# A seven-product GELU matmul kernel: B's operands kept in DRAM, two products of four groups split again, A's rows weighed by ScalarE

**Chip, cores, metric.** One core of a Trainium2 chip. The metric is the device time of one execution in microseconds (us), median of several.

## The reference

```python
def reference(a, b):            # a, b: 4096 x 4096 float32
    x = np.matmul(a, b)
    return 0.5 * x * (1 + np.tanh(np.sqrt(2 / np.pi) * (x + 0.044715 * x**3)))
```

## The kernel before

The kernel forms each 2 x 2 block product with seven products instead of eight (the Winograd form of Strassen's scheme), in f16 with fp32 sums in PSUM. There are 16 groups: four row blocks of A by four column blocks of B. A product is four steps (`q`) of 16 matmuls of 512 columns. Its operands are blocks of A and B, or sums of two, made by DVE two steps ahead.

```python
PRODUCTS = [("M3", "Y", "11", ("12", "22", 1)), ("M5", "X", ("11", "12", -1), "22"), ...]   # 7 of them

def make_sums(gi, s, q):                       # DVE: operand sums, 128 x 2048 f16 each
    ...
    t = pool.tile([P, 4 * NC], F16, name=tag, tag=tag, bufs=AHEAD + 1)      # AHEAD = 2
    nc.vector.tensor_tensor(out=x, in0=y, in1=z, op=...)

def keep(tag, src, bufs):                      # ScalarE copies a finished bank out of PSUM
    t = pool.tile([P, NC], F32, name=tag, tag=tag, bufs=bufs)
    nc.scalar.copy(out=t[:, :], in_=src[:, :])
```

After M5, M7 and M1 the next product goes on adding into the same PSUM banks, so TensorE must wait until ScalarE has copied each bank out (`m`, `x`).

A's rows come through two staging buffers. GpSimd issues the load (fp32 to f16), DVE turns the chunk into `aT`, and the buffer is free.

```python
s = pool.tile([P, NX, RUN], F16, name="stage", tag="stage", bufs=2)          # load_a
nc.vector.transpose(dst[:, :, x, :], src[:, :, x, :])                        # turn_a
```

The scheme is exact enough only for tame inputs, so the kernel also sums the squares of A's rows and B's columns and falls back to plain products if they are out of bounds. Before, ScalarE squared resident tiles and DVE added the squares.

## Time and profile before

| | before |
|---|---|
| time, median of 3 | 1579.29 us |
| span of the profiled run | 1577.1 us |
| TensorE busy, granted clock | 1567.7 us (99%), 0.999 |
| DVE, ScalarE, GpSimd busy | 78%, 33%, 34% |
| TensorE's waits, all added | 4.2 us |

Two more views. First the waits between other engines (columns: engine, tile and line, what it waited for; total us, times, longest).

```profile
POOL stage L186 <- DVE aT L161: 178.0, 16, 56.7
ACT square L207 <- DVE energy L431: 130.7, 96, 4.7
...
DVE aT L161 <- DMA stage<-in_a_dram: 39.9, 14, 10.8
```

A staging buffer is waited for until DVE has turned it, never until ScalarE has done anything. DVE stands 39.9 us in all at turns whose rows are not there, and TensorE does not feel it. Second, the DMA issues (count, size of one, median us from issue to landing).

```profile
bR<-in_b_dram POOLq DMA_DIRECT2D x832, 128.0 KB, 5.2
...
stage<-in_a_dram POOLq DMA_DIRECT2D x112, 256.0 KB, 6.8
```

### The profile page before, as it was taken

The numbers are of one execution on the slowest core, as the hardware profiler recorded it, in microseconds if no ns is written. First come the engines' busy times: TensorE is split into PE (matmuls) and PEld (weight loads), VectorE is DVE, ScalarE is ACT, GpSimd is POOL, SyncE is SP. The second block draws the span as 40 slices with busy tenths as digits, with TensorE's granted clock in tenths as the row PEclk, the third lists the DMA queues.
The fourth block names the chain that finished last, engine by engine and source line by source line (L and its number), as shares of the span: only waits on it lengthen the run. The fifth ranks groups of instructions, "written<-read, shape, count | busy, mean of one in ns | idle before, by whom it ended". The sixth has DMA issues, their size and how long they took to land. (4 is left out here: it accounts for less than half of the span.)

```text
span 1577.1 us, 19678 instructions
## 1 busy us (share of the span) xinstructions
PE 1567.7 (99%) x7246; PEld 709.6 (45%) x7246; DVE 1233.7 (78%) x1381; ACT 518.0 (33%) x710; POOL 537.7 (34%) x980
## 2 busy tenths in 40 slices
PE   9999999999999999999999999999999999999998
PEld 4444444444444444444444444444444444444443
DVE  1698888967787888895778778887687778988775
ACT  1036445311122545531111344542211145364111
POOL 7753442420234144341124413245011443314400
PEclk9999999999999999999999999999999999999999
DMA  9999884882968378686597937679468885747802
GB/s 173 198 215 189 132 162 79 161 162 48 193 106 158 87 131 160 108 179 115 87 161 117 186 72 142 146 113 182 79 121 146 134 160 93 151 105 134 161 28 82
DMA packets 225047, 211.13 MB, mean 134 GB/s; under 512 B 20144, under 2 KB 192176, under 8 KB 224944
## 3 DMA queue, kind: packets, MB, share of 16 engines
q0 software_dynamic: 187648, 142.67, 61.7%
q1 hardware_dynamic: 37296, 67.13, 11.8%
q8 instruction: 59, 0.97, 0.2%
q14 instruction: 44, 0.36, 0.1%
HBM read 285.22 MB, written 67.11 MB: 223 GB/s over the span
## 5 line engine op out<-in xcount | busy, mean ns | idle before, releaser
L331 PEld LDWEIGHTS <-aS 128*128 128x128 f16 x4960 | 485.3, 98 | 587.2 <-issue 2.2
L186 POOL DMA_DIRECT2D bR<-in_b_dram x832 | 447.6, 544 | 700.0 <-DVE bS L302 329.7
L302 DVE TENSOR_TENSOR aS<-aT 128x2048 f16<-128x2048 f16 (+1 forms) x312 | 376.1, 1212 | 151.0 <-PE accX L331 114.5
L331 PE MATMUL accX<-bS,aS 128*128 128x512 f16 x1984 | 431.1, 379 | 0.0
L302 DVE TENSOR_TENSOR bS<-bR 128x2048 f16<-128x2048 f16 x310 | 376.1, 1218 | 69.3 <-PE accX L331 58.5
L331 PEld LDWEIGHTS <-aT 128*128 128x128 f16 x1984 | 194.2, 98 | 234.8 <-issue 0.8
L422 ACT ACTIVATE y<-y 128x512 f32<-128x512 f32 x192 | 118.5, 630 | 351.8 <-DVE y L431 351.4
L331 PE MATMUL accY<-bS,aS 128*128 128x512 f16 x992 | 216.7, 379 | 1.8 <-DVE y L431 1.8
L331 PE MATMUL accY<-bS,aT 128*128 128x512 f16 x992 | 216.9, 379 | 0.5 <-DVE bS L302 0.5
L331 PE MATMUL accX<-bS,aT 128*128 128x512 f16 x992 | 216.7, 379 | 0.0
L331 PE MATMUL accX<-bR,aS 128*128 128x512 f16 x992 | 216.7, 379 | 0.0
L331 PE MATMUL accY<-bR,aS 128*128 128x512 f16 x992 | 216.7, 379 | 0.0
L186 POOL DMA_DIRECT2D stage<-in_a_dram x144 | 89.9, 630 | 249.0 <-DVE aT L161 178.0
L431 DVE TENSOR_TENSOR energy<-energy,square 128x1024 bf16<-128x1024 bf16 x240 | 164.4, 685 | 9.5 <-ACT square L207 5.7
L395 ACT COPY x<-accX 128x512 f32<-128x512 f32 x128 | 74.9, 585 | 224.3 <-PE accX L331 224.3
L207 ACT ACTIVATE square<-aT 128x1024 bf16<-128x1024 f16 x120 | 123.4, 1051 | 70.6 <-DVE energy L431 70.2
L207 ACT ACTIVATE square<-bR 128x1024 bf16<-128x1024 f16 x120 | 123.0, 1050 | 62.5 <-DVE energy L431 60.5
L161 DVE STREAM_TRANSPOSE aT<-stage 128x2048 uint32<-128x2048 uint32 (+1 forms) x37 | 74.6, 2017 | 46.0 <-DMA stage<-in_a_dram 39.9
L395 ACT COPY m<-accX 128x512 f32<-128x512 f32 x60 | 34.7, 579 | 215.7 <-PE accX L331 213.6
L422 ACT ACTIVATE y<-accX 128x512 f32<-128x512 f32 x64 | 38.2, 597 | 100.1 <-PE accX L331 99.9
L431 DVE TENSOR_TENSOR x<-accX,x 128x512 f32<-128x512 f32 x64 | 44.0, 691 | 21.8 <-ACT y L422 19.1
L431 DVE TENSOR_TENSOR y<-accY,m 128x512 f32<-128x512 f32 x60 | 39.9, 687 | 12.5 <-ACT m L395 12.4
(38 smaller groups left out, 344.9 us busy)
## 6 DMA issues: line engine op xcount, KB each, us to landing
bR<-in_b_dram POOLq DMA_DIRECT2D x832, 128.0 KB, 5.2
out_dram<-y SPq DMA_DIRECT2D x256, 256.0 KB, 5.7
stage<-in_a_dram POOLq DMA_DIRECT2D x112, 256.0 KB, 6.8
stage<-in_a_dram POOLq DMA_DIRECT2D x32, 128.0 KB, 5.1
row<-seen_d SPq DMA_DIRECT2D x2, 1.5 KB, 4.2
seen_d<-seen SPq DMA_DIRECT2D x1, 3.0 KB, 7.4
```

What stands on the lines that cost most here:

```text
L161: nc.vector.transpose(dst[:, :, x, :], src[:, :, x, :])
L186: nc.gpsimd.dma_start(out=dst, in_=src)
L207: nc.scalar.activation(t[:, :], src, ACT.Square)
L302: nc.vector.tensor_tensor(out=x, in0=y, in1=z, op=ALU.add if o[2] > 0 else ALU.subtract)
L331: nc.tensor.matmul(acc[:, :], sa[:, j // 2, i * P : (i + 1) * P, j % 2], sb[:, j, :], start=start and j == 0, stop=stop and j == 3, skip_g ...
L395: nc.scalar.copy(out=t[:, :], in_=src[:, :])
L422: nc.scalar.activation(y[:, :], src[:, :], ACT.Gelu_apprx_tanh)
L431: nc.vector.tensor_tensor(out=o[:, :], in0=x[:, :], in1=y[:, :], op=op)
```

## The change

Intent: TensorE is the bound, so take matmuls away. M3 and M5 of groups 11, 13, 14 and 15 become seven products of half size each. That needs DVE time for more sums and joins, so DVE is relieved in two ways: B's operands, once made, are written to DRAM in groups 1 to 5 and fetched from group 6 on; and A's rows are weighed by ScalarE straight from the staging buffer, with no DVE work. The core of the diff:

```diff
+SPLIT_GROUPS = (11, 13, 14, 15)
+CHECK_GROUP = 9
+TURNS = ((2, 2), (3, 1), (5, 2), (6, 1), (7, 0), (7, 3), (8, 2), (9, 1))
...
+    def weigh_rows(mb, quad, c, xs):
+        s = staged[mb, quad, c]
...
+        for x in xs:
+            nc.scalar.activation(
+                weighed[mb, quad, c][:, :RUN], s[:, x, :], ACT.Square, accum_out=weighed[mb, ih][:, k, x : x + 1]
+            )
...
+    def keep_operand(key, x, src):
+        nc.sync.dma_start(out=dst, in_=src)             # a sum, or a raw block, to DRAM
...
+    def multiply_split(gi, s, p):                       # one of seven parts: 2 row tiles x 8 matmuls x 256 columns
...
+            elif p == "3":
+                joined(join("2"), region(chain, "12", r), join("2"), ALU.subtract)
+                joined(join("2"), region(chain, "11", r), join("2"), ALU.add)
...
+    def stage_block(mb, turns, turned=True):
+        for (quad, c), n in zip(chunks, turns):
+            do(n - 3, load, (load_a, (mb, quad, c)))
+            if turned:
+                do(n, turn_a, mb, quad, c)
+            for x in range(3):
+                do(n + x, weigh_rows, mb, quad, c, list(range(NX))[x * 6 : (x + 1) * 6])
...
+    stage_block(0, [first_step[CHECK_GROUP] + 3 + 4 * x for x in range(len(chunks))], turned=False)
...
+    def fetch(key, x):
+        t = split_tiles[key] = ring_tile(x, "bK")
+        nc.gpsimd.dma_start(out=t, in_=kept_unit(*key[1:])[:, :])      # 1 MB, into a ring of eight places
```

A's first block is read a second time in group 9 only to be weighed. Groups 6, 7, 9 and 10 ("makers") also form the split operands of B and store them.

## The prediction

> **What bounds the kernel now.** I read the page's busy shares first.
>
> ```profile
> PE 1567.7 (99%) x7246; PEld 709.6 (45%) x7246; DVE 1233.7 (78%) x1381; ACT 518.0 (33%) x710; POOL 537.7 (34%) x980
> ```
>
> TensorE is busy for all but 9 us of the span, the next engine is at 78%. A busy TensorE could still be a slow one, so next come the windows by stage (columns: window, its length, then busy us and instructions of PE, PEld, DVE, ACT, POOL, granted clock, DMA share, GB/s).
>
> ```profile
> 100.00:200.00 100.00, 97.69 (x453) 44.12 (x452) 86.42 (x106) 48.48 (x62) 43.07 (x81) 1.00 0.89 168
> 1300.00:1400.00 100.00, 100.00 (x465) 45.37 (x464) 85.37 (x103) 49.80 (x62) 34.40 (x64) 1.00 0.67 127
> ```
>
> Only the stretch from 100 to 200 us has TensorE gaps after the start (2.3 us); from 200 to 1500 us it is solid at clock 1.00, although DVE reaches 86%. The waits of TensorE say the same; this is its whole list (columns: who waits on what; total us, times, longest).
>
> ```profile
> PE accY L331 <- DVE y L431: 1.8, 1, 1.8
> PE accX L343 <- DVE table L583: 1.4, 1, 1.4
> PE accY L331 <- DVE bS L302: 0.5, 1, 0.5
> PE accY L362 <- DMA bR<-in_b_dram: 0.5, 1, 0.5
> ```
>
> Waits come to 4.2 us in all. So neither DVE nor DMA sets the end; the number and pace of matmuls do. The pace is read from the timeline of TensorE late in the run, where each line is one product of group 15 (start, us, line, count).
>
> ```profile
> 1502.65 13.98 PE L331 MATMUL accX<-bS,aS 128*128 128x512 f16 x64
> 1516.47 13.98 PE L331 MATMUL accX<-bS,aT 128*128 128x512 f16 x64
> ...
> 1557.91 13.98 PE L331 MATMUL accX<-bS,aS 128*128 128x512 f16 x64
> ```
>
> From 1502.65 to 1516.47 are 13.82 us for 64 matmuls: **215.9 ns each** (the 379 ns in the groups is a latency, they overlap). 7200 such matmuls are 1554 us of the 1577.1 us span; the other 23 us are the warm-up (13), the 4 us of waits and the tail, all of which the change leaves alone. A group of seven products is 448 x 215.9 = 96.7 us.
>
> **What the Trainium skill says.** (1) "TensorE: Matmul & The Clock Gate", Back-to-back issue gap: the isolated warm gap is N/2.4 + 2.5 ns, so 215.8 ns for N=512, which this trace confirms (215.9), and 109.2 ns for N=256, of which no instruction exists in this trace. The same section gives about 81 ns for N=128 in a stream that also loads weights, so a pair of load and matmul can pass faster than 109 ns. That matters, because the record of one weight load here is 98 ns, near the 109. (Its other figure, 131 ns for N=512, the trace contradicts.) (2) "VectorE: DVE Perf Modes", Why PSUM operands drop a tier: fp32 with a PSUM operand runs at one element a cycle; at that page's 0.96 GHz, halving 512 columns takes 267 ns off. The trace agrees that PSUM gives no worse than SBUF in fp32: 691 and 682 ns. (3) "PSUM — Partial Sum Buffer", The four PSUM rules: DVE and ACT writes do not set has_written. This explains why the first matmul of each bank in the lower half is issued 512 wide: the later products must add onto quarters that ACT wrote. No run so far shows it. (4) "DMA: Bandwidth & Descriptors", Why small descriptors are slow: a fixed cost per packet. The kept operands come as rows of 8 KB a partition against 2 KB rows of fp32 now. This trace has no 8 KB rows.
>
> **The change part by part.**
>
> *Seven products for M3 and M5 in groups 11, 13, 14, 15.* This is the only part that takes work from TensorE. Removed per group: 2 products x 64 = 128 matmuls of 512 columns, 128 x 215.9 = 27.64 us. Added: 2 products x 7 parts x 2 row tiles x 8 = 224 matmuls, 4 of them still 512 wide. 220 x 109.2 + 4 x 215.9 = 24.02 + 0.86 = 24.89 us (estimate from the gap formula above). Gain 2.75 us a group, **11.0 us in four groups**, all on the path, since TensorE has no gaps there. That is 0.7% of the time; this bounds what the change can give, apart from the 2.3 us of gaps at 100 to 200 us.
>
> *What the split costs DVE and ACT.* Per split product 8 joins of 256 fp32 columns with PSUM operands, estimate 691 - 267 = 424 ns: 16 a group, 6.8 us. A's sums for the pair go from 4 to 14 (10 quarter sums, 4 sums of the whole block for M5) of 1.22 us (row aS<-aT), so +12.2 us. ACT gets 8 small copies, about 0.4 us each. In the pair's 24.9 us DVE then has 10 x 1.22 + 6.8 + 4 outputs x 0.69 = 21.8 us, or 26.7 with the block sums, which may be made up to six steps ahead. So DVE is near full there, but it has the earlier product's 13.8 us to run ahead in, and B's sums are gone from it.
>
> *B's operands kept in DRAM for groups 6 to 15.* Removed: 20 sums x 10 groups x 1.218 = 244 us of DVE; and 512 of the 832 loads of B. Added: 4 blocks x 10 sums to make the split operands, 49 us of DVE; stores of 4 x 14.7 MB (28 halves of 0.5 MB each) while the first groups run and 4 x 7.3 MB in the makers, on the SP queue; and 6 x 14 + 4 x 17 = 152 fetches of 1 MB. Software-queue bytes go from 142.7 to about 243 MB (42 B, 42 A, 159 kept), the hardware queue's from 67 to about 155. A usual group fetches 14.7 MB in 96.7 us, 152 GB/s; the pair, 7 MB in 24.9 us, about 295 GB/s unless the ring of eight 1 MB places has run ahead. On TensorE's path: nothing, if all land in time.
>
> *A weighed by ACT.* Gone: 120 squares and 8 first ones of A on ACT (132 us), 120 sums on DVE x 0.685 = 82 us, and 8 weighings x 1.95 = 16 us. Added: 4 blocks x 8 chunks x 16 = 512 ACT instructions of 256 elements. From 1050 ns at 1024 elements and 630 at 512, the slope is 0.82 ns, so about 420 ns each: 215 us. Also one block of A is read a second time (8.4 MB landed).
>
> *Sums.* DVE 1234 - 244 + 49 + 49 (A sums) + 27 (joins) - 98 = about 1017 us (65%). ACT 518 - 132 + 215 + 13 = about 614 us (39%). TensorE about 1557 us. Of these only the last is on the path: 1579.3 - 11.0 = 1568.3 us. I add 1.7 us for new waits, because the split chain is tight: the seventh part needs a quarter that DVE joins after the fifth, with two steps of 1.75 us between. That makes **1570 us**.
>
> **The rivals.**
>
> (a) *A weight load cannot hide under 256 columns.* For: 98 ns of record against 109 of matmul. Against: the skill's 81 ns. If a pair took 125 ns, 224 would take about 28 us, the same as now, and the time would be 1579; at 118 ns about 1573. I give a visible loss here 15%.
>
> (b) *DVE's joins become TensorE's bound in the pairs.* For: 22 to 27 us of DVE work in 24.9 us, in order, and steps half as long as before. Against: DVE at 86% left no TensorE gap from 200 us on, and sums are made ahead. One to two us a pair would make 1572 to 1576.
>
> (c) *DMA.* The stores of kept operands fall into groups 1 to 5, where the DMA share is already 0.9 and TensorE's only late gaps are; bS has three buffers, which now stay taken until a store has read them. For: 15 MB more in a 97 us group, behind output stores on the same queue. Against: rows of 4 to 8 KB, and two to three steps (7 to 10 us) against 5.7 us to landing. A lasting stall here would make 1575 to 1590; I give that 10%.
>
> (d) *The freed DVE time itself gives time.* DVE loses about 217 us net, but TensorE waits on it for 2.3 us only, in group 1, where nothing is relieved. I expect 0 from it.
>
> **Range and chances.** The best case is all parts at 109 ns and no new wait, 1568; with the old gap of 2.3 us gone too, 1566. The likely case has 0 to 4 us of new waits. Weight on (a), (b) and (c) lengthens the upper side only: 1567 to 1577. Faster by 2% would need 31.6 us, three times what TensorE sheds: 0.01. Slower by 2% needs stalls of over 40 us: 0.03.
>
> **What would show it.** In the profile after: matmuls of 256 columns about 109 ns apart (a pair's stretch near 25 us instead of 27.6, with 2.75 us less per split group and an unsplit group still 96.7); TensorE still about 99% busy; DVE near 65%, ACT near 39%; joins near 0.42 us and the weighing near 0.42 us. The prediction is wrong if the 256-column matmuls are spaced 115 ns or more, if waits of TensorE on joins or on fetched operands sum to over 5 us, or if groups 1 to 5 take over 97.5 us each.

## The result

The changed kernel ran in 1634.76 us (median of 4, 1627.86 to 1643.15) against 1579.59 us, correct. The ratio is 1.0351 (95% interval 1.0301 to 1.0401): **slower by 3.5%**, where a gain of 0.6% was forecast. A ratio is the mean time of one kernel's runs over that of the other's runs of the same rounds, so not quite the ratio of the medians quoted. By a rule of 2%, of all versions below only e5 is "slower" as well; e3 (1.0194) is unclear and the others count as the same, so smaller differences rest on the medians and intervals given, and runs of different rounds are compared only roughly.

The page of the kernel after, busy shares:

```profile
PE 1572.6 (96%) x7630; PEld 748.9 (46%) x7630; DVE 1033.0 (63%) x1189; ACT 653.2 (40%) x1638; POOL 366.6 (22%) x652
```

DVE is relieved as forecast (1033 us, forecast 1017), TensorE is less busy in share and yet the span is 58 us longer. First the part that was to gain. The timeline of TensorE over the pair of group 11, after (start, us, line, columns, count):

```profile
1142.99 3.87 PE L483 MATMUL accY<-bK,aS 128*128 128x512 f16 x32
1146.69 1.91 PE L483 MATMUL accY<-bK,aT 128*128 128x256 f16 x16
1148.44 3.87 PE L483 MATMUL accX<-bK,aS 128*128 128x512 f16 x32
...
1167.87 13.98 PE L401 MATMUL accX<-bK,aS 128*128 128x512 f16 x64
```

From 1142.99 to 1167.87 are 24.88 us for the pair, forecast 24.89. Sixteen 256-column matmuls pass in 1.75 us (1146.69 to 1148.44), 109.4 ns each, with no wait on a join (DVE's adding of quarter results). (The first line merges 2 wide and 30 narrow ones under one form.) So the split works, and the loss is elsewhere. The stretches of 100 us show where (columns as in the prediction):

```profile
400.00:500.00 100.00, 85.06 (x376) 37.36 (x374) 73.96 (x79) 69.36 (x209) 22.03 (x38) 0.93 0.84 198
...
800.00:900.00 100.00, 88.84 (x392) 39.06 (x390) 47.45 (x46) 61.18 (x216) 18.74 (x31) 0.93 1.04 253
900.00:1000.00 100.00, 90.44 (x420) 40.83 (x418) 43.17 (x44) 39.62 (x126) 17.16 (x29) 0.97 0.93 254
...
1400.00:1500.00 100.00, 100.00 (x574) 55.88 (x573) 62.30 (x78) 20.08 (x38) 9.67 (x18) 1.00 0.62 231
```

The stretches that lose most are those in which A's rows are staged and weighed (groups 3/4, 7/8, 9, 11/12), at a lower granted clock; the last stretch shown, with one split pair and no staging, is solid at clock 1.00. TensorE's waits after:

```profile
PE accX L401 <- ACT x L513: 22.8, 4, 11.7
PE accX L401 <- ACT m L513: 12.1, 3, 5.4
PE accX L401 <- DVE aS L365: 8.3, 1, 8.3
PE accY L401 <- DVE y L549: 7.5, 2, 5.7
```

With the rest they add to 57.1 us, 53 more than before. Of the 53, 34.9 us are waits on ScalarE's copies `x` and `m` out of PSUM. TensorE's busy time is 1572.6 us, where 1567.7 - 11 was due; these 16 us are matmuls at a lower clock (from 400 to 500 us, 376 matmuls took 226 ns each instead of 215). 53 + 16 - 11 = 58 us, the whole difference of the spans.

Why is a 0.6 us copy late? The longest wait, in group 9, is read from the timeline (in brackets: idle time before, and what ended it):

```profile
978.82 2.58 POOL L206 DMA_DIRECT2D stage<-in_a_dram  x4
981.39 1.12 POOL L760 DMA_DIRECT2D bK<-k_M  x2
...
998.40 0.42 ACT L228 ACTIVATE scrap<-stage 128x256 bf16<-128x256 f16 x1 [15.88 <-DMA stage<-in_a_dram]
...
1001.52 2.03 ACT L513 COPY x<-accX 128x512 f32<-128x512 f32 x4
1002.11 0.69 DVE L549 TENSOR_TENSOR x<-x,x 128x512 f32<-128x512 f32 x1 [20.77 <-ACT x L513]
1002.13 2.29 PE L401 MATMUL accX<-bK,aT 128*128 128x512 f16 x5 [11.69 <-ACT x L513]
```

GpSimd asks for the rows at 978.8 us; they land only at 998.4 us, beside fetches of 1 MB. ScalarE's next instruction is a weighing of these rows. It stands 15.9 us, then does six weighings (3.1 us), and only then the copies, which could have been done at about 990. The Trainium skill, "TensorE: Matmul & The Clock Gate" (the specifications at its head), says that ScalarE's, VectorE's and GpSimdE's queues are strictly first in, first out; this trace agrees: a copy of finished data stood 11.7 us behind a weighing that waited for a DMA. The windows then show what a wait does to the clock (next to last but two: granted clock):

```profile
976.00:1002.00 26.00, 14.44 (x67) 6.45 (x66) 3.59 (x3) 9.39 (x36) 7.58 (x13) 0.85 1.13 310
1002.00:1006.00 4.00, 3.87 (x10) 1.38 (x10) 3.78 (x6) 3.87 (x14) 1.45 (x3) 0.50 1.01 428
1006.00:1018.00 12.00, 12.00 (x53) 5.25 (x52) 3.99 (x6) 4.99 (x21) 3.17 (x5) 0.93 1.26 298
```

The same page ("Why this matters for your kernels") warns of gaps over some 3 us: the clock falls to half. Here it was 0.50 for the first 4 us after the wait, and the product that followed took 16.54 us instead of 13.82. The length of a wait alone did not decide it: after one of 2.50 us (in group 1) 32 matmuls took 8.75 us instead of 7.07, after one of 3.11 us (in group 4) 64 took 13.97, no longer than after none.

DVE is caught in the same way, at a turn:

```profile
809.41 2.31 DVE L181 STREAM_TRANSPOSE aT<-stage 128x2048 uint32<-128x2048 uint32 x1 [9.61 <-DMA stage<-in_a_dram]
...
814.62 16.59 PE L401 MATMUL accY<-bK,aS 128*128 128x512 f16 x64 [5.72 <-DVE y L549]
```

(These two come from the timelines of DVE and of TensorE.) TensorE's wait of 8.3 us, in group 4, shows the whole chain, from the timelines of GpSimd, DVE and TensorE:

```profile
431.36 2.54 POOL L206 DMA_DIRECT2D stage<-in_a_dram  x4 [10.63 <-ACT scrap L228]
...
439.03 2.31 DVE L181 STREAM_TRANSPOSE aT<-stage 128x2048 uint32<-128x2048 uint32 x1 [8.13 <-DMA stage<-in_a_dram]
...
443.11 12.88 PE L401 MATMUL accX<-bR,aS 128*128 128x512 f16 x48 [8.33 <-DVE aS L365]
```

GpSimd stood 10.6 us until ScalarE gave up the buffer; the rows landed 7.7 us after the issue, and DVE and TensorE had stood for them. The waits between the engines, added up, are to be held against those of before:

```profile
POOL stage L206 <- ACT scrap L228: 186.9, 18, 28.8
...
DVE aT L181 <- DMA stage<-in_a_dram: 91.4, 16, 10.8
ACT scrap L228 <- DMA stage<-in_a_dram: 78.6, 11, 15.9
```

The staging buffers now wait for ScalarE, not DVE, and ScalarE and DVE both stand at rows that are not there. A load also takes longer:

```profile
bK<-k_M POOLq DMA_DIRECT2D x124, 1024.0 KB, 9.8
...
stage<-in_a_dram POOLq DMA_DIRECT2D x144, 256.0 KB, 10.2
```

10.2 us from issue to landing against 6.8 before, and the change asks for the rows three steps ahead: 3 x 3.45 = 10.4 us. (The diff shows that before it was 3 to 11 steps, by chunk.) The runs below tell whose traffic it is: the same median is 6.7 us where A is weighed and nothing kept (e3), 13.4 and 12.9 us where B's operands are kept and nothing is weighed (e7, e1). And ScalarE's groups show a cost that was not in the forecast:

```profile
L228 ACT ACTIVATE scrap<-stage 128x256 bf16<-128x256 f16 x512 | 212.8, 416 | 100.5 <-DMA stage<-in_a_dram 78.6 <-issue 6.8 <-DVE stat_a L236 0.8
...
L228 ACT ACTIVATION_READ_ACCUMULATOR scrap<-stage 128x1 f32 x512 | 95.6, 187 | 0.0
```

Each weighing of 416 ns (forecast 420) is followed by a read of the accumulator of 187 ns; in the timeline one row takes 0.54 us. A chunk of 16 rows is 8.6 us of the 10.4 us that three steps give. In groups 3 and 4 the change also puts the squares of B's block 3 there, one of 1.05 us in each step: 8.6 + 3 x 1.05 = 11.8 us of work in 10.4 us, before any copy or output.

### The profile page after: what moved, and what is told of

The parts are those of the page before. It is cut to its first block, busy times and chain, and to the rows that moved or that the text cites. A ratio compares the mean times of both kernels' runs of the same rounds, so it can differ in the third digit from the quotient of the medians. Undisturbed runs are those within 1.5% of the kernel's fastest.

```text
span 1635.2 us, 21115 instructions
## 1 busy us (share of the span) xinstructions
PE 1572.6 (96%) x7630; PEld 748.9 (46%) x7630; DVE 1033.0 (63%) x1189; ACT 653.2 (40%) x1638; POOL 366.6 (22%) x652
## 5 line engine op out<-in xcount | busy, mean ns | idle before, releaser
L401 PE MATMUL accX<-bK,aS 128*128 128x512 f16 x1664 | 366.6, 383 | 15.7 <-ACT m L513 9.3
L763 DVE TENSOR_TENSOR aS<-aT 128x2048 f16<-128x2048 f16 x204 | 241.2, 1215 | 82.8 <-PE accX L401 60.9
L401 PE MATMUL accY<-bK,aS 128*128 128x512 f16 x1280 | 280.7, 382 | 5.7 <-DVE y L549 5.7
L228 ACT ACTIVATE scrap<-stage 128x256 bf16<-128x256 f16 x512 | 212.8, 416 | 100.5 <-DMA stage<-in_a_dram 78.6
L206 POOL DMA_DIRECT2D bR<-in_b_dram x320 | 172.9, 543 | 230.4 <-DMA bR<-in_b_dram 100.8
L401 PE MATMUL accX<-bS,aS 128*128 128x512 f16 x704 | 154.4, 381 | 5.9 <-ACT x L513 3.1
L365 DVE TENSOR_TENSOR aS<-aT 128x2048 f16<-128x2048 f16 (+1 forms) x112 | 133.9, 1200 | 36.4 <-PE accX L401 25.9
L401 PE MATMUL accX<-bK,aT 128*128 128x512 f16 x640 | 142.5, 384 | 11.7 <-ACT x L513 11.7
L365 DVE TENSOR_TENSOR bS<-bR 128x2048 f16<-128x2048 f16 x110 | 133.7, 1218 | 17.7 <-PE accX L401 16.8
L228 ACT ACTIVATION_READ_ACCUMULATOR scrap<-stage 128x1 f32 x512 | 95.6, 187 | 0.0
## 6 DMA issues: line engine op xcount, KB each, us to landing
stage<-in_a_dram POOLq DMA_DIRECT2D x144, 256.0 KB, 10.2
```

Source lines behind the costliest of these rows:

```text
L206: nc.gpsimd.dma_start(out=dst, in_=src)
L228: nc.scalar.activation(weighed[mb, quad, c][:, :RUN], s[:, x, :], ACT.Square, accum_out=weighed[mb, ih][:, k, x : x + 1])
L365: nc.vector.tensor_tensor(out=x, in0=y, in1=z, op=ALU.add if o[2] > 0 else ALU.subtract)
L401: nc.tensor.matmul(acc[:, :], sa[:, j // 2, i * P : (i + 1) * P, j % 2], sb[:, j, :], start=start and j == 0, stop=stop and j == 3, skip_g ...
L763: nc.vector.tensor_tensor(out=t, in0=y, in1=z, op=ALU.add if op > 0 else ALU.subtract)
```

## The experiments

Theory W: weighings stand in ScalarE's queue in front of PSUM copies and wait for rows that land late. Rivals: the kept operands' traffic or the joins alone (K); ScalarE's time alone, in any order (W2).

### One part at a time

**e1_no_weigh**: no weighing; the table is filled with a constant, so the check is void on purpose, but the outputs stay right.

```diff
-            for x in range(3):
-                do(n + x, weigh_rows, ...)
+        nc.vector.memset(stats["a"][:, :], 1024.0)
```

> The change without ScalarE's weighing of A's rows (its table of row energies is filled with a constant, the extra read of A's first block in group 9 stays, the outputs stay right). Theory W, the weighing stands in front of ScalarE's PSUM copies and waits for late staged rows: TensorE's waits of some 55 us and the slow clock after them vanish, 1567 to 1573 us. Rival K, the traffic of the kept operands or the joins of the split products stall TensorE by themselves: 1600 us or more.

Measured: 1593.61 us (ratio 1.0088) against 1578.47. Neither theory alone: 41 us of the loss go, 15 us over the kernel before stay, some 25 over the 1568 that the split should give. TensorE's waits were 22.7 us, the largest on DVE and on a fetch:

```profile
PE accY L401 <- DVE y L549: 7.8, 2, 6.1
PE accY L401 <- DMA bK<-k_M: 3.6, 1, 3.6
```

**e2_weigh_ones**: the same 512 weighings in the same places, of a constant tile, holding no staging buffer (check void on purpose).

```diff
-                weighed[mb, quad, c][:, :RUN], s[:, x, :], ACT.Square, accum_out=...
+                s[:, :], s[:, :], ACT.Square, accum_out=...        # s: a tile of ones
```

> The same 512 ScalarE weighings in the same places of the program, but of a constant tile, so that they wait for no staged row and hold no staging buffer. If the harm is the waiting for staged rows (W1): 1568 to 1580 us. If it is ScalarE's own time, 0.54 us a row beside copies, squares and outputs (W2): 1605 us or more.

Measured: 1606.24 us. By the letter W2's forecast is met and W1's failed; but both had been drawn before e1 was known, which without any weighing is at 1593.61 us. Against that it splits the 41 us: 12.6 us (1606.24 - 1593.61) are ScalarE's own time in front of the copies; the other 28.5 us (1634.76 - 1606.24, from different rounds) come with the staged rows, their late landing and the buffers held.

**e3_weigh_alone**: no kept operands, no split; only the weighing with its new staging order.

```diff
-SPLIT_GROUPS = (11, 13, 14, 15)
+SPLIT_GROUPS = ()
-    N_RAW = NNB + 2
+    N_RAW = len(groups)          # B loaded and summed in every group; nothing stored
...
```

> A's weighing on ScalarE with its new staging order alone: B loaded and summed in every group as before, nothing kept in DRAM, no split. If the late rows need the traffic of the kept operands (W1 by contention): 1578 to 1590 us. If the two staging buffers, held until ScalarE has weighed them, are enough by themselves: 1610 us or more.

Measured: 1609.69 us (1.0194). So 31 us are lost without any of the kept traffic; its waits are again on ScalarE's copies:

```profile
PE accX L398 <- ACT m L510: 14.3, 3, 7.5
```

The bound of 1610 us for "by themselves" was met but for 0.3 us, and the forecast for the rival (1590 at most) failed: contention is not needed for a loss. But the trace shows that held buffers are not enough by themselves either: in groups 7/8 and 11/12, with the same staging and weighing, TensorE waits 0.3 us in all. The waits stand in two places. In groups 3/4 (11.2 us) ScalarE goes without a pause through weighings and the squares of B's block 3 and stands for no row in the 20 us before the longest wait (6.0 us; e2, which needs no rows, has the same 6.0 us there). In groups 9/10 (14.0 us) it stands 21.3 us for the rows of the second read, which GpSimd asks for only at 921.2 us, behind B's loads in its queue.

**e5_no_check_group**: the whole change without the second read and weighing in group 9 (one line taken out, that part of the table a constant).

> The whole change, less only the second read and weighing of A's first block in group 9. Theory W: that group's one wait of 11.7 us and its slow restart go, about 14 us less, 1618 to 1624 us. Rival K: no more than 5 us less.

Measured: 1619.51 us, 15.3 us less, as theory W said; the wait of 11.7 us is gone from the list.

**e7_kept_alone**: e1 with `SPLIT_GROUPS = ()`.

> B's operands kept in DRAM alone: no weighing of A, no split pairs (split operands still made and stored). If the three parts add up, this is e1 (1593.6 us) plus the split's 11 to 14 us: 1604 to 1608 us, so the kept operands alone lose 25 us or more against the kernel before. If the split is what the traffic hurts: within 5 us of 1579 us.

Measured: 1602.48 us (1.0150) against 1580.14. The kept operands alone, with the new staging order, lose 22 us, a little less than the 25 of the forecast. The split alone is worth 1602.48 - 1593.61 = 8.9 us here and 13.5 us between t4 and t4_no_split below; the profile's 4 x 2.75 = 11 lies between. Added up: +22 (kept), +31 (weighed), -11 (split) give 42 us of the 55; the remaining 13 us are parts hurting each other. TensorE's waits by place, from the timelines of the profiled runs (us), show where:

| groups | before | change | e2, own time | e3, weighed alone | e7, kept alone |
|---|---|---|---|---|---|
| 0 to 2 | 4.2 | 7.5 | 6.1 | 4.1 | 5.6 |
| 3/4 | 0 | 16.5 | 9.8 | 11.2 | 3.0 |
| 7/8 | 0 | 11.2 | 9.1 | 0 | 6.3 |
| 9/10 | 0 | 11.7 | 2.4 | 14.0 | 2.6 |
| 11/12 | 0 | 10.2 | 3.0 | 0.3 | 1.2 |

ScalarE's own time costs most in groups 3/4, where B's squares stand with it. The excess of the change over e3 and e7 together is in groups 7/8 and 11/12 (13.6 us), where the weighing is harmless until the kept traffic makes its rows late: in front of the longest wait there (6.4 us, group 11) ScalarE had stood 10.5 us for rows. That is read from the traces, not from a run made for it.

**e6_no_weigh_early**: e1 with `do(n - 3, load, ...)` made `do(n - 5, load, ...)`.

> The kernel without weighing (e1), with one number changed: A's staged rows are asked for five steps (17 us) before they are turned instead of three (10.4 us). Theory L: what e1 still loses against 1568 us is DVE standing at a turn whose rows land late in the kept operands' traffic, and TensorE behind it. Then 1568 to 1578 us. Rival: the traffic itself, fetched operands late or DVE short of time, costs it: within 5 us of e1's 1593 us.

Measured: 1587.73 us, 5.9 us less than e1, where theory L claimed 16 to 26; the rival's 5 us are nearly met. e1's four runs spread over 10 us and were made in another round (intervals 1.0060 to 1.0117 for e1, 1.0038 to 1.0071 here), so even the 5.9 us is not clear of noise. Late rows at a turn are at most one part of what the kept operands cost, not the whole.

### Re-timed versions

These keep all of the change's work and alter only when it is placed.

**t1_stretch**: one chunk in four steps, loads four steps ahead, weighing one step after the turn.

```diff
-TURNS = ((2, 2), (3, 1), (5, 2), (6, 1), (7, 0), (7, 3), (8, 2), (9, 1))
+TURNS = ((2, 2), (3, 2), (5, 2), (6, 2), (7, 2), (8, 2), (9, 2), (10, 2))
-            do(n - 3, load, ...)   ...   do(n + x, weigh_rows, ...)
+            do(n - 4, load, ...)   ...   do(n + 1 + x, weigh_rows, ...)
```

> The whole change with the staging stretched to one chunk in four steps instead of three, loads four steps ahead, the weighing one step behind the turn. Theory: late rows and held buffers cause the waits, so most of the 55 us go: 1575 to 1595 us, what is left being in group 9, where the second read meets a group that makes split operands. Rival, ScalarE too slow in any order: over 1605 us.

Measured: 1595.68 us (median; one run at 1607). 39 us less than the change, a hair above the range named; of what stayed, two waits on fetches are in group 9, as said (4.8 and 2.6 us), but they are 7.4 of TensorE's 26 us of waits: not "what is left".

**t2_lag**: also the second read of A's first block moved to groups 13 and 14, and half of the squares of B's block 3 moved to before the staging.

```diff
-    stage_block(0, [first_step[CHECK_GROUP] + 3 + 4 * x for x in range(len(chunks))], turned=False)
+    stage_block(0, [first_step[g] + 17 + 4 * x for g in (13, 14) for x in range(len(chunks) // 2)], turned=False)
```

> As t1_stretch, and the second read of A's first block moved from group 9 to groups 13 and 14, after their split pairs, and the squares of B's block 3 done half in the first ten steps of group 3, before staging begins. If staging is the whole cause: 1568 to 1576 us, faster than the kernel before.

Measured: 1581.80 us (1.0024). 53 of the 55 us are gone by order alone, with ScalarE as busy as in the change (657 us). This refutes W2 as a bound: its time costs only where copies stand behind it. But it is not the 1568 to 1576 us forecast.

**t3_early**: t2 with loads five steps ahead and the weighing in the turn's own step (`n - 5`, `n + x`).

> As t2_lag, but loads five steps ahead and the weighing in the turn's own step. 1568 to 1576 us; better than t2_lag if the turn's wait for late rows costs more than ScalarE's.

Measured: 1590.57 us, 9 us worse than t2. Seven waits on copy `x` (9.3 us) came back: a weighing right at the turn would stand in front of the copies more often, but the lead of the loads was changed with it, so this is argued and not shown. The forecast failed.

**t4_all, t5_leads, t4_no_split**: t2 with the first four chunks asked for 7 or 8 steps ahead, B's squares outside the staging; t4 also queues stores of kept sums after the outputs of the step; t4_no_split has `SPLIT_GROUPS = ()`.

> t2_lag with three more moves that remove no work: the first four chunks of A are asked for seven or eight steps ahead, as both staging buffers are free then; B's block 3 is squared outside the staging steps; the stores of kept sums are queued after the outputs of the same step. If staging order was all that hid the gain: TensorE's waits under 8 us, 1567 to 1573 us, 0.4 to 0.7% faster than the kernel before. If the traffic holds it: 1578 us or more.

> t4_all without the move of the stores behind the outputs: 2 to 3 us slower than t4_all if the wait in group 1 comes from outputs standing behind stores on the SP queue, equal if not.

> t4_all without the split pairs: 11 us slower than t4_all (four times 2.75 us), if 256-column matmuls pass at 109 ns and the joins cost TensorE nothing; within 3 us if the joins or the fetches eat the gain.

Measured: t4 1582.16 us (1.0012, interval 0.9996 to 1.0028), t5 1581.42, t4_no_split 1595.70 (1.0108). Stores behind outputs change nothing. The split is worth 13.5 us where 11 were forecast (the runs of the two versions spread over 8 and 11 us); no wait of TensorE in t4's profile is on a join. The forecast of 1567 to 1573 failed.

**t6_squares, t7_maker**: t5 with B's squares out of steps 9 to 11 of group 3; t7 also makes block 2's split operands in group 8 (`and g != 7` in the choice of makers).

> t5_leads, with the squares of B's block 3 kept out of steps 9 to 11 of group 3, where t5's largest wait (3.6 us, TensorE on a PSUM copy behind squares and weighings) stands. 3 to 5 us off the profiled span, 1574 to 1579 us, so 0 to 0.3% faster than the kernel before; no change if another wait steps into its place.

> t6_squares, with block 2's split operands made in group 8 instead of group 7. If t5's wait of 2.6 us on a fetch, whose place waits for a store of a split operand, comes from the stores meeting the staged rows of group 7: 2 to 4 us less than t6. If group 8's staging meets them as well: equal.

Measured: t6 1579.15 us (1.0003, 0.9981 to 1.0025), t7 1578.55 us (1.0002, 0.9989 to 1.0015). Level with the kernel before; t7 is not told from t6. The forecast for t6 failed (span 1577.4 us in t5, 1578.1 in t6): the wait on `x` went, and waits on B's sums grew to 5.3 us. In t7's profile TensorE is busy 1559.0 us, 8.7 less than before, and waits 12.1 us, 7.9 more: the gain of the split is just spent.

**t8_beside, t9_beside_defer**: t7 with chunks placed so that no weighing falls into the last step of M5, M7 or M1, and asked for as soon as a buffer should be free (leads 8, 8, 7, 6, 4, 5, 6, 5); t9 with the stores behind the outputs.

> t7_maker, with the chunks of A placed so that no weighing falls into the last step of M5, M7 or M1, whose PSUM copies TensorE waits for, and each chunk asked for as soon as its staging buffer is free. If order on ScalarE's queue is what is left: the waits after 700 us go (3.3 us and the slow restart behind it), 1571 to 1576 us, 0.2 to 0.5% faster than the kernel before. If late rows remain: equal to t7 within 2 us.

> t8_beside, with the stores of kept sums queued after the outputs of the same step. Equal to t8 within 2 us, as between t4 and t5; 2 us or more less if the sum buffers held by stores in groups 1 to 5 are what remains.

Measured: t8 1580.57 us (1.0007), t9 1579.36 (0.9997). The waits on copies are gone as meant (0.2 us in all in t8), but the forecast of 1571 to 1576 failed: another has stepped in, 4.3 us on a fetch. The timeline of GpSimd in t8:

```profile
843.75 2.54 POOL L208 DMA_DIRECT2D stage<-in_a_dram  x4 [21.63 <-ACT scrap L230]
846.28 0.57 POOL L762 DMA_DIRECT2D bK<-k_M  x1
847.51 1.61 POOL L762 DMA_DIRECT2D bK<-k_M  x3 [0.66 <-DVE aT L183]
```

A load asked for too early waits 21.6 us in GpSimd's queue for ScalarE to give up the buffer, with the fetches behind it.

**t10_raw_first, t11_raw_first_7**: t8 with leads 8, 8, 6, 5, 4, 4, 4, 4, and the split operands that are plain copies stored first; t11 with block 2 made in group 7.

```diff
-            for s in (0, 1) for k, p in enumerate("1346725")
+            for s in (0, 1) for k, p in enumerate("2513467")
```

> t8_beside, with the last chunks of A asked for four steps ahead instead of five or six (so that GpSimd's queue does not stand at a staging buffer that ScalarE still holds, with the fetches behind it), and the split operands that are plain copies stored first. If that queue is what is left: t8's wait of 4.3 us on a fetch and its slow restart go, 1572 to 1576 us. If another wait takes its place: 1578 us or more.

> t10_raw_first, with block 2's split operands made in group 7 again. Equal within 2 us, if the place of making does not matter once the order is right; 2 us or more slower if the stores meet the staged rows of group 7.

Measured: 1601.52 and 1602.27 us: worse by 21 us. The wait on a fetch is gone as meant, but the new order of makes brings one wait of 2.8 to 5.7 us in each of the four maker groups. In t10, DVE's waits, a line that t8's list does not have at all:

```profile
DVE bS L765 <- DMA k_split<-bS: 46.8, 9, 11.5
```

Sums now stand before a buffer that a store still reads. As two things were changed at once, this pair tells the leads' effect only by the vanished wait. Groups 7 and 8 are equal as places of making.

No version beat the kernel before: the lowest ratio is t9's 0.9997 (0.9982 to 1.0011).

## Why the prediction was wrong, point by point

- **Bound and pace**: right. TensorE at 215.9 ns a matmul, no slack elsewhere that gives time.
- **The split**: right to 0.01 us a pair (24.88 us), 109.4 ns a matmul, joins 421 to 429 ns (forecast 424). Rivals (a) and (b), weight load and joins, did not occur.
- **Bytes and instructions**: right. The software queue moved 243.3 MB (forecast 243), the hardware queue 155.2 (155), 152 fetches. What rows of 8 KB gain by themselves, point (4), no run isolates.
- **DVE's sum**: 1033 us, forecast 1017. ScalarE's: 653 us, forecast 614; the missing term is the accumulator's read, 512 x 187 ns = 95.6 us of records, partly overlapped with the next row.
- **"A weighed by ACT"**: here is the step that failed. It was worked out as time on an engine at 33% and then put aside with "Of these only the last is on the path". The position in ScalarE's queue was not asked for: weighings come before the copies that release PSUM banks, they wait for a DMA, and they hold the staging buffers that DVE alone held before. Alone this costs 31 us (e3), all of it where something else meets it: B's squares in ScalarE's queue (groups 3/4) or a busy GpSimd queue (the second read, groups 9/10). By ScalarE's time alone it is 13 us (e2 against e1).
- **"On TensorE's path: nothing, if all land in time"** (kept operands): also failed. Rival (c) named traffic, but put it into groups 1 to 5 and onto bS. Alone it costs 22 us (e7), and of the waits it adds there, 4.4 us are in groups 1 to 4 and 10 us in groups 7 to 12, where rows asked for three steps ahead (10.4 us) met a median landing of 13.4 us.
- **The signs of being wrong**: one came true. Groups 1 to 5 were to take at most 97.5 us each; group 4 took 116 us. That came less from the stores that rival (c) feared than from ScalarE's queue. No wait was on a join, and none on a kept fetch.
- **Slow clock after waits**: no term at all for it; 16 us.
- **Slower by over 2%**: given 0.03. The range was drawn as a few us of waits on a sum of busy times, though the change rewrote the order of three queues.

What stays open: the new staging order by itself (leads of three steps throughout, other turns) was never run without either the weighing or the kept operands beside it. e3 and e7 both carry it, so what it costs is counted twice in their sum, and which part of the kept operands' 22 us is traffic and which is order is not known; e6 gives the order's leads about 6 us, not clear of noise. The interaction of 13 us is placed, but not tested.

## What to carry to other kernels

Moving work to an idle engine is safe only if its place in that engine's queue is: ask what instruction stands behind it, what it waits for, and which buffer it keeps. When TensorE is at 99%, a copy that releases a PSUM bank is part of the critical path, so neither a wait for a DMA nor a full load of other work should stand in front of it. A wait can cost more than its length, since the clock may fall after it: here 53 us of waits came with 16 us of slow matmuls, in t2 11.5 us with 1.3. A load's lead is to be set against the landing time under the new traffic (10.4 us against 6.7 in e3 and 13.4 in e7), but not so early that it blocks its own queue on a buffer still held (21.6 us in t8).

## What the Trainium skill lacked or had wrong

- "ScalarE: Activation LUTs" says that an activation can give an accumulator output, but no cost: here each is a further instruction of 187 ns, and one row of 256 columns takes 0.54 us instead of the 0.42 us of the activation's record.
- "TensorE: Matmul & The Clock Gate", Back-to-back issue gap: 131 ns for N=512 in a stream with weight loads is contradicted (215.9 ns); the isolated formula holds in such a stream, also at N=256 (109.4 ns with weight loads of 98 ns beside it).
- "DMA: Bandwidth & Descriptors" gives a fit of 2.0 us plus bytes over 436 GB/s for one DMA (an estimate of 4.4 us for 1 MB; its own table has 6.15 us for 1 MB): under this kernel's traffic the median landing was 9.8 us for the 124 fetches of kept products and 5.9 us for the 28 of split operands. For load the page has only the latency of HBM, no landing time.
- "Perfetto Trace Analysis" takes occupancy as the measure for ScalarE and VectorE: here TensorE waited 57 us, nearly all of it for ScalarE at 40% and DVE at 63%; between the change and t2_lag ScalarE's busy time is equal (653 and 657 us) and the times differ by 53 us. The page does say to look for an engine's gaps and for what blocks it, and that unsaturated engines can cause bubbles on others; what stands in front of a PSUM copy in its queue it does not name.
